# Eight half-tile sums of each group, and the two small operations of a row tile's scale, issued on GpSimd instead of VectorE

## The chip, the cores and the metric

The kernel runs on one core of a Trainium2 chip. The core has TensorE (PE, matrix products into PSUM), VectorE (DVE), ScalarE (ACT), GpSimd (POOL) and SyncE (SP, which issues the DMA transfers here). Each engine runs its own instructions in order, and instructions on different engines are tied together by semaphores. The metric is device microseconds for one execution of the whole kernel. The kernel before took 1449.78 us as the median of 2 runs (1449.72 to 1449.84).

## The reference

```python
# x: (8, 2048, 2048) float32, w: (2048, 2048) float32
def reference(x, w):
    cs = np.cumsum(x, axis=1)
    diff = cs - np.concatenate([zeros, cs[:, :-1, :]], axis=1)
    return np.matmul(diff, w).astype(np.float32)
```

A running sum along the second axis followed by the difference of neighbours gives x back, so what has to be computed is the product of x, seen as a matrix of 16384 rows by 2048 columns, with w.

## The kernel before

**Tiling.** The rows of x are cut into 128 row tiles of 128 rows. The first tiles are multiplied plainly in bf16 (the head), while w is being read. From row tile 4 on, the work is in f16: four row tiles make a group, called g, h, k and l (rows g, g+2, g+1, g+3), and the group's product with w is done with a scheme of Strassen's kind: sums of blocks of x times sums of blocks of w, with fewer products and more additions. The first f16 group (`group_plain`) and the next (`group_half`) are written out by hand. The other 29 groups are made by the class `Group` and form a steady loop.

**One group in the loop.** The half of a row tile that belongs to one half of the inner dimension is a `Part` of 128 x 1024 f16 numbers in the tiles x (`turned_x`). The eight sums that the change concerns combine the parts in place: for the pairs g,k and h,l they are S1 (A21 + A22), S2 (S1 - A11), S4 (A12 - S2) and S3 (A22 - S2, called after S4 in the plan). There are seven large products P1 to P7. P6 and P7 read S2 and S3 directly: each is eight steps (`P6g.0` to `P6g.3`, `P6h.0` to `P6h.3`) of four matmuls, issued from line 609. P1 to P5 go one level deeper: each has four small sums of 128 x 512 (`P1.s1` to `P5.s3`, line 599, 0.42 us each on VectorE) and seven quarter products of four matmuls (line 628), with one or two sums of weights made for them just in time in the tile `flow` (`P2.fp4`, `P5.fp5` and so on, line 955, 128 x 2048). P5 reads S1, P3 reads S4. All of them together are 51 steps of four matmuls in a group. ScalarE (`keep`, line 636) and VectorE (`add`, line 639) gather the products from PSUM into the f32 results c, which SyncE stores (`put`).

**How a row tile comes in.** `load` (SyncE, into one of five f32 buffers F), `weigh` (ScalarE, line 125: the sum of the absolute values of a row), `scale` (lines 142 and 144: a maximum with a tiny number and its reciprocal, 128 x 1), `unit` (GpSimd, line 150, 128 x 2: what the results are multiplied by), `narrow` (ScalarE, line 164: f32 to f16, times the scale, in place), `turn` (SyncE, line 177: two transposing DMAs into the parts). There is one place in x for each of g, h, k and l, so `turn` of the next group waits until TensorE has read the last of this one.

**The order.** Each engine's instructions go in the order in which the kernel asks for them (`after` chains them). In the loop that order is one list written out by hand, `ORDER`, in which every step stands once with the group that it is of (`S1.g+1` is of the group one ahead of `P4.p6+0`). It is one order for all engines, and each engine follows its own part of it. GpSimd's part of the list is, in the kernel before, `unit.h unit.g unit.l unit.k`. VectorE's part around the sums is

```
... P2.s1 P2.s2 P1.m2 P2.s4 S1.g S2.g add.C21h1.q scale.l add.C11g0.v P2.fp4 P2.s3 add.C11g1.q S4.g
add.C11h1.e add.C11h1.q add.C21h0.x S3.g add.C11h0.q P5.fp5 S1.h P5.s1 scale.g P5.s2 P5.s4 S2.h P5.s3
add.C11g1.e P5.fp4 P5.m1 S4.h P3.s1 P3.s2 P5.m2 S3.h P3.s4 P3.s3 add.C22g0.x P3.fp2 add.C12h1.z scale.h ...
```

and TensorE's part in the same stretch is

```
... P1.p3 P1.p4 P2.p2 P6g.0 P2.p6 P6g.1 P2.p5 P6g.3 P2.p7 P6g.2 P5.p1 P2.p4 P2.p3 P7g.0 P7g.1 P5.p2 P5.p5
P5.p6 P6h.2 P6h.1 P6h.3 P6h.0 P5.p7 P7g.2 P7g.3 P5.p4 P5.p3 P7h.0 P3.p2 P3.p1 P7h.2 ...
```

Of the kernel before, what the change touches and what calls it, by code (L numbers as in the profile page):

```python
# [10 lines left out]
def kernel(  # L11
# [6 lines left out]
    nc = tc.nc  # L18
    P = 128
# [10 lines left out]
    f32 = mybir.dt.float32  # L30
    ADD = mybir.AluOpType.add
    SUB = mybir.AluOpType.subtract
    MUL = mybir.AluOpType.mult
    MAX = mybir.AluOpType.max
# [5 lines left out]
    TINY = 1e-34  # L40
# [11 lines left out]
    const = ctx.enter_context(tc.tile_pool(name="const", bufs=1))  # L52
# [19 lines left out]
    uw = const.tile([P, 2], f32, name="uw")  # L72
    uinv = const.tile([P, 2], f32, name="uinv")

    waste = const.tile([P, NH], mybir.dt.uint8, name="waste")
    F = const.tile([P, 5, NH], f32, name="F")
    turned_x = [
# [10 lines left out]
    def after(engine, ask):  # L88
        if engine in last:
            with tc.issue_after(last[engine].ins):  # L90
                said = ask()
        else:
            said = ask()
        last[engine] = said[-1] if isinstance(said, tuple) else said
        return said
# [38 lines left out]
    def scale_of(t):  # L134
        if t < END:
            m2 = sums_of.pop(t)
            m, s = (m2[:, i : i + 1] for i in (2, 3))
            u = m2[:, 4:6]
            scales[t], unit[t] = s, u
            after(  # L140
                "dve",
                lambda: nc.vector.tensor_scalar(m, m2[:, :1], m2[:, 1:2], TINY, ADD, MAX),  # L142
            )
            after("dve", lambda: nc.vector.reciprocal(s, m))  # L144
            sizes[t] = m

    def unit_of(t):
# [38 lines left out]
    with ExitStack() as head:  # L186
# [195 lines left out]
        for ko in range(1, KO - 1):  # L382
# [3 lines left out]
            q = (ko + 1) // KQ  # L386
# [3 lines left out]
            for r in range(PLAIN):  # L390
                if turning and r in (0, PLAIN - 1):
                    a = r // 2
# [23 lines left out]
        def bring(ko):  # L416
            fetch(1, ko)
            cast(1, ko)
            measure(1, ko)
            if ko == AHEAD:  # L420
                scale_of_w(0)
            if ko > AHEAD:
                turn_left(1)
            if ko == 10:
                load(PLAIN, 0)
                load(PLAIN, 1)
                weigh(PLAIN)
                scale_of(PLAIN)
            if ko == 11:
                narrow(PLAIN)  # L430
# [51 lines left out]
        for k in range(KH):  # L482
            block(B12, 0, 1, k, "dve")
            if k == 1:
                scale_of(PLAIN + 2)
            if k % 2:
                if k // 2:
                    finish_row(k // 2)
# [12 lines left out]
        turn(PLAIN + 2)  # L501
        weigh(PLAIN + 1)
        scale_of(PLAIN + 1)
        unit_of(PLAIN + 1)
        narrow(PLAIN + 1)
# [32 lines left out]
    S1 = [S1_all[:, ds(2 * i, 2), :] for i in range(2)]  # L538
    inner = alone([P, 20, NB], f16, "inner")
    flow = alone([P, 4, NB], f16, "flow")  # L540
    S1 = [Part(t) for t in S1]
# [55 lines left out]

    def total(dst, p, q, op):
        after("dve", lambda: nc.vector.tensor_tensor(dst.all, p.all, q.all, op))  # L599


    def steps(to, a, b, first, pieces):
# [59 lines left out]
    def sums_in(a, b, to):  # L662
        a11, a12, a21, a22 = a.half(0), a.half(1), b.half(0), b.half(1)
        s1, s2, s3, s4 = to

        def one():
            total(s1, a21, a22, ADD)
            total(s2, s1, a11, SUB)

        def two():  # L670
            total(s3, a11, a21, SUB)
            total(s4, a12, s2, SUB)

        return one, two, (a11, a12, a22, s1, s2, s3, s4)
# [300 lines left out]
    class Group:  # L975
# [120 lines left out]
        def plan(self):  # L1096
# [25 lines left out]
            v, q, e = "2v", "2q", "2e"  # L1122
# [18 lines left out]

            for a, b in ("gk", "hl"):
                (A11, A12), (A21, A22) = half[a], half[b]
                self.step(f"S1.{a}", total, A21, A21, A22, ADD)
                self.step(f"S2.{a}", total, A11, A21, A11, SUB)
                self.step(f"S4.{a}", total, A12, A12, A11, SUB)
                self.step(f"S3.{a}", total, A11, A22, A11, SUB)

            self.whole("P6", T2, half["g"][0], half["h"][0], *x)
            for n, c in zip(x, ("C12h0", "C12h1", "C12g0", "C12g1")):  # L1150
# [8 lines left out]
            q, e = "3q", "3e"  # L1159
# [26 lines left out]
            q, e = "4q", "4e"  # L1186
# [149 lines left out]
```

## Time and profile before

| what | value |
|---|---|
| median of the runs | 1449.78 us (1449.72 to 1449.84) |
| span of the profiled execution, first to last instruction | 1447.4 us |
| time around the span (median less span) | 2.4 us |
| TensorE busy | 1437.9 us, 99% |
| VectorE busy | 1319.0 us, 91% |
| ScalarE busy | 970.5 us, 67% |
| GpSimd busy | 43.8 us, 3% |
| mean granted TensorE clock | 1.000 |
| one group in the loop | 44.04 us |

The profiled execution has its span as its own time; the runs' median stands 2.4 us above it. The page of the profile gives busy time by engine, then the costliest groups of instructions by source line, with the mean duration of one and the idle time of the engine just before them. The timeline of an engine lists its instructions in order of time with start and duration, neighbours of one kind merged ("x2"); a tiny overlap of neighbours is the pipeline. Steps are found in it by counting along the lists above, since the loop repeats every 44.04 us.

### The profile page before, as it was taken

Reading aid. Unit: us, or ns where it says so; the run is one execution under the profiler, and the core shown is the slowest. Engines: PE = TensorE matmul, PEld = TensorE weight load, DVE = VectorE, ACT = ScalarE, POOL = GpSimd, SP = SyncE. Lnnn points to the kernel's source line nnn. Section 1 sums busy time; section 2 is a strip of 40 time slices with the busy share of each in tenths; the row PEclk is TensorE's granted clock in tenths of the full one; section 3 lists DMA queues with packets and bytes.
Section 4 is the critical chain, followed back from the end, with each engine's and each line's share of the span. In section 5 each row is a group of like instructions: output and inputs, shape, how many; then the busy total and the mean of one; then the engine's idle time right before and its main releaser. Section 6 shows DMA issues by size and latency. Waiting matters only on the chain.

```text
span 1447.4 us, 20191 instructions
## 1 busy us (share of the span) xinstructions
PE 1437.9 (99%) x6686; PEld 651.6 (45%) x6692; DVE 1319.0 (91%) x2310; ACT 970.5 (67%) x1472; POOL 43.8 (3%) x130
## 2 busy tenths in 40 slices
PE   8999999999999999999999999999999999999998
PEld 4444444444444444444444444444444444444443
DVE  4899899999999999999999999999999999999998
ACT  6987566666666776666666667666667766666662
POOL 0011000000000000000000000000000000000000
PEclk9999999999999999999999999999999999999999
DMA  9999788899888898888899888998878998889973
GB/s 363 368 257 298 200 234 232 239 253 253 226 224 239 238 254 245 231 233 236 248 247 232 234 238 233 262 240 234 228 234 240 252 234 239 226 242 248 255 200 127
DMA packets 378199, 351.58 MB, mean 243 GB/s; under 512 B 274800, under 2 KB 274800, under 8 KB 377968
## 3 DMA queue, kind: packets, MB, share of 16 engines
q1 hardware_dynamic: 378096, 350.31, 86.5%
q8 instruction: 52, 0.85, 0.2%
q14 instruction: 51, 0.42, 0.1%
HBM read 150.99 MB, written 134.22 MB: 197 GB/s over the span
## 4 chain that ended last, share of the span: by engine, by line
PE 97%; DMA 2%; DVE 0%; SPq 0%; issue 0%; DVEq 0%
PE b L628 62%; PE b L609 33%; PE b L304 2%; DMA W<-in_w_dram 2%; DMA W<-in_x_dram 0%; DVE c L639 0%; PE b L464 0%; SPq L225 0%; DVE wb L267 0%; SPq L259 0%; DVEq L267 0%; DVEq L639 0%
## 5 line engine op out<-in xcount | busy, mean ns | idle before, releaser
L639 DVE SCALAR_TENSOR_TENSOR c<-b,of,c 128x512 f32<-128x512 f32 x790 | 573.6, 746 | 71.1 <-PE b L628 61.4
L609 PE MATMUL b<-W,x 128*128 128x512 f16 x2144 | 507.1, 379 | 0.0
L636 ACT ACTIVATE c<-b,of 128x512 f32<-128x512 f32 x492 | 312.7, 680 | 220.2 <-PE b L628 113.8
L628 PE MATMUL b<-W,x 128*128 128x512 f16 x1904 | 454.9, 379 | 0.0
L164 ACT ACTIVATE F<-F,of 128x1024 f16<-128x1024 f32 x246 | 282.3, 1148 | 175.6 <-DVE of L144 173.4
L628 PEld LDWEIGHTS <-x 128*128 128x128 f16 x2500 | 244.6, 98 | 295.4 <-issue 1.0
L609 PEld LDWEIGHTS <-x 128*128 128x128 f16 x2144 | 209.7, 98 | 253.3 <-issue 0.5
L125 ACT ACTIVATE waste<-F 128x1024 uint8<-128x1024 f32 x246 | 259.3, 1054 | 8.3 <-DMA F<-in_x_dram 6.2
L628 PEld LDWEIGHTS <-inner 128*128 128x128 f16 x1644 | 160.8, 98 | 194.0
L628 PE MATMUL b<-W,inner 128*128 128x512 f16 x940 | 241.2, 379 | 0.0
L599 DVE TENSOR_TENSOR x<-x,x 128x1024 f16<-128x1024 f16 (+1 forms) x390 | 227.1, 583 | 3.3
L628 PE MATMUL b<-flow,x 128*128 128x512 f16 x584 | 149.9, 379 | 0.0
L628 PE MATMUL b<-inner 128*128 128x512 f16 x472 | 121.1, 379 | 0.0
L955 DVE TENSOR_TENSOR flow<-W 128x2048 f16<-128x2048 f16 x87 | 105.7, 1215 | 0.0
L1053 DVE TENSOR_TENSOR b<-b,c 128x512 f32<-128x512 f32 x116 | 80.4, 693 | 12.7 <-PE b L628 12.7
L150 POOL TENSOR_SCALAR of<-uw,of 128x2 f32<-128x2 f32 x124 | 42.6, 357 | 1299.6 <-DVE of L142 717.1
L955 DVE TENSOR_TENSOR flow<-W,inner 128x2048 f16<-128x2048 f16 x58 | 70.7, 1220 | 0.0
L1046 ACT COPY c<-b 128x512 f32<-128x512 f32 x58 | 33.4, 576 | 51.2 <-PE b L628 51.2
L304 PE MATMUL b<-wb,xP 128*128 128x512 bf16 x234 | 53.2, 379 | 2.2 <-ACT wb L265 1.1
L599 DVE TENSOR_TENSOR inner<-x 128x512 f16<-128x512 f16 x117 | 49.3, 421 | 3.1 <-DMA x<-F 1.0
L1046 ACT COPY b<-b 128x512 f32<-128x512 f32 x87 | 51.2, 589 | 0.2 <-PE b L628 0.2
L599 DVE TENSOR_TENSOR inner<-x,inner 128x512 f16<-128x512 f16 x117 | 49.2, 421 | 2.0
(68 smaller groups left out, 517.5 us busy)
## 6 DMA issues: line engine op xcount, KB each, us to landing
F<-in_x_dram SPq DMA_DIRECT2D x246, 512.0 KB, 5.2
out_dram<-c SPq DMA_DIRECT2D x492, 256.0 KB, 3.0
W<-in_w_dram SPq DMA_DIRECT2D x32, 512.0 KB, 8.4
W<-in_x_dram SPq DMA_DIRECT2D x16, 256.0 KB, 7.8
x<-F SPq DMA_TRANSPOSE x246, 3.4
out_dram<-o SPq DMA_DIRECT2D x5, 256.0 KB, 7.0
out_dram<-wb SPq DMA_DIRECT2D x5, 256.0 KB, 7.0
xP<-in_x_dram SPq DMA_DIRECT2D x1, 1024.0 KB, 6.4
```

Of the source, the lines that this page charges most:

```text
L125: lambda: nc.scalar.activation(waste, where[t][i], ABS, scale=1.0 / ROW, accum_out=sums_of[t][:, i : i + 1],),
L150: after("pool", lambda: nc.gpsimd.tensor_scalar(u, uw, m, None, MUL))
L164: lambda: nc.scalar.activation(narrowed(t)[:, ds(i * NH, NH)], where[t][i], COPY, scale=s),
L304: lambda: nc.tensor.matmul(ps[r][n], xP[:, r, ko, :], wb[h, ko][:, ds(n * NB, NB)], start=(ko == 0), stop=(ko == KO - 1),),
L599: after("dve", lambda: nc.vector.tensor_tensor(dst.all, p.all, q.all, op))
L609: said = nc.tensor.matmul(to[n], a[k], b[k][:, n, :], start=(first and k == 0), stop=(k == KH - 1), skip_group_check=True,)
L628: said = nc.tensor.matmul(to, a[k], b[k], start=(first and k == 0), stop=(k == 3), skip_group_check=True)
L636: after("act", lambda: nc.scalar.activation(c, p, COPY, scale=u))
L639: after("dve", lambda: nc.vector.scalar_tensor_tensor(c, p, u, c, MUL, ADD))
L955: after("dve", lambda: nc.vector.tensor_tensor(in_twos(to), x, y, op))
L1046: after("act", lambda: nc.scalar.copy(c, p))
L1053: after("dve", lambda: nc.vector.tensor_tensor(t, p, s, ADD))
```

## The change

The eight sums S1 to S4 of the loop are asked of GpSimd by a new helper `total_aside`, at the same places of `ORDER`. The sums of the two groups written out by hand stay on VectorE. The two operations of `scale` go to GpSimd too, for every row tile from the first f16 one on, and the reciprocal is written as the power -1, with a constant column of -1.

```diff
+    minus = const.tile([P, 1], f32, name="minus")
+    nc.vector.memset(minus, -1.0)
...
             after(
-                "dve",
-                lambda: nc.vector.tensor_scalar(m, m2[:, :1], m2[:, 1:2], TINY, ADD, MAX),
+                "pool",
+                lambda: nc.gpsimd.tensor_scalar(m, m2[:, :1], m2[:, 1:2], TINY, ADD, MAX),
             )
-            after("dve", lambda: nc.vector.reciprocal(s, m))
+            after(
+                "pool",
+                lambda: nc.gpsimd.tensor_tensor(s, m, minus, mybir.AluOpType.pow),
+            )
...
+    def total_aside(dst, p, q, op):
+        after("pool", lambda: nc.gpsimd.tensor_tensor(dst.all, p.all, q.all, op))
...
-                self.step(f"S1.{a}", total, A21, A21, A22, ADD)
-                self.step(f"S2.{a}", total, A11, A21, A11, SUB)
-                self.step(f"S4.{a}", total, A12, A12, A11, SUB)
-                self.step(f"S3.{a}", total, A11, A22, A11, SUB)
+                self.step(f"S1.{a}", total_aside, A21, A21, A22, ADD)
+                self.step(f"S2.{a}", total_aside, A11, A21, A11, SUB)
+                self.step(f"S4.{a}", total_aside, A12, A12, A11, SUB)
+                self.step(f"S3.{a}", total_aside, A11, A22, A11, SUB)
```

GpSimd's part of the list becomes `unit.h unit.g S1.g S2.g scale.l unit.l unit.k S4.g S3.g S1.h scale.g S2.h S4.h S3.h scale.h scale.k`, where each `scale` is two instructions.

## The prediction

> **What bounds the kernel now.** I read the page first, then the busy time of each engine over the whole loop and over one group.
>
> ```profile
> span 1447.4 us, 20191 instructions
> PE 1437.9 (99%) x6686; PEld 651.6 (45%) x6692; DVE 1319.0 (91%) x2310; ACT 970.5 (67%) x1472; POOL 43.8 (3%) x130
> ```
>
> ```profile
> 160.00:1400.00 1240.00, 1240.00 (x5746) 562.00 (x5744) 1149.98 (x2030) 832.12 (x1265) 30.24 (x111) 1.00 0.87 238
> 635.84:679.88 44.04, 44.04 (x206) 19.96 (x205) 40.79 (x72) 29.61 (x45) 1.09 (x4) 1.00 0.89 239
> ```
>
> Columns of the second fence: window, length, then busy time of TensorE, its weight loads, VectorE, ScalarE and GpSimd, then granted clock. In 1240 us of the loop TensorE is busy 1240.00 us at clock 1.00, so it never stalls: whatever VectorE saves there saves nothing, and every delay that reaches a matmul is added in full, in each of 29 groups of 44.04 us. All idle time of TensorE in the span is 1447.4 - 1437.9 = 9.5 us, less than the 29 us (2%) that a measurement of this kernel can tell from no change. So the question is only which sum comes too late, and by how much.
>
> **What is moved.** The groups of instructions, shapes kept apart (count, busy time, mean ns of one, idle before):
>
> ```profile
> L164 ACT ACTIVATE F<-F,of 128x1024 f16<-128x1024 f32 x246 | 282.3, 1148 | 175.6 <-DVE of L144 173.4
> L599 DVE TENSOR_TENSOR x<-x,x 128x1024 f16<-128x1024 f16 x240 | 164.1, 684 | 1.1
> L150 POOL TENSOR_SCALAR of<-uw,of 128x2 f32<-128x2 f32 x124 | 42.6, 357 | 1299.6 <-DVE of L142 717.1
> L142 DVE TENSOR_SCALAR of<-of 128x1 f32<-128x1 f32 x124 | 25.4, 205 | 4.4 <-ACT waste L125 4.3
> L144 DVE RECIPROCAL of<-of 128x1 f32<-128x1 f32 x124 | 20.3, 164 | 4.3
> ```
>
> 232 of the 240 sums move (29 groups of 8; the other 8 are in the groups written by hand), and 124 scales. VectorE loses 8 x 0.684 + 4 x (0.205 + 0.164) = 6.9 us of its 40.79 per group. That is worth nothing by itself, since TensorE is full.
>
> **What one sum costs on GpSimd (S).** The trace has none. From below the nearest row is VectorE's own 0.684 us. From above I take four times ScalarE's row of one operand of 1024 numbers, 4 x 1.148 = 4.6 us. I choose S = 2.3 us, twice that row: GpSimd's small operations (0.357 us for 128x2 on the average, 0.28 undisturbed, below) cost more than VectorE's (0.205), so it is nearer to the engine that takes one number at a time, and a sum has two operands where ScalarE's instruction has one. The Trainium skill, "GPSIMD Engine Reference", section 3.1, gives 4497 ns for an f32 sum of 2048; half of it, 2.25 us as an estimate, would make the sum below 4.7 us a group in place of 4.9. The scale's two operations I put at 0.3 us each, the row of 128x2 without its waits; the power is not in the trace, and lies between nothing and 1.15 us (ScalarE's long row), 0.85 us more a scale at worst.
>
> **Do GpSimd and VectorE hinder each other?** GpSimd's timeline beside VectorE's, early and in the loop:
>
> ```profile
> 87.47 1.37 POOL L150 TENSOR_SCALAR of<-uw,of 128x2 f32<-128x2 f32 x1 [8.67 <-DVE of L142]
> ...
> 658.30 0.55 POOL L150 TENSOR_SCALAR of<-uw,of 128x2 f32<-128x2 f32 x2 [21.75 <-DVE of L142]
> ```
>
> ```profile
> 87.49 3.68 DVE L591 TENSOR_TENSOR W<-W 128x1024 f16<-128x1024 f16 x6
> ...
> 658.17 0.16 DVE L144 RECIPROCAL of<-of 128x1 f32<-128x1 f32 x1
> 658.28 0.75 DVE L639 SCALAR_TENSOR_TENSOR c<-b,of,c 128x512 f32<-128x512 f32 x1
> ```
>
> The same GpSimd operation takes 0.28 us (two in 0.55) beside an `add`, whose big operand b is in PSUM, and 1.37 us beside sums of two tiles in SBUF: it got through after the second of six. So GpSimd waits for VectorE's two-tile sums, and not for its adds. Whether VectorE's sums wait for GpSimd in turn, no row shows; I forecast that they do, for the whole of S, and price the other case as a rival. The Trainium skill, "SBUF — State Buffer", section "Who interferes with whom", has it so: the pair of ports is taken by whichever comes first for its whole instruction and the other is blocked. The row above agrees for one direction; by this rule the sum is 4.9 us a group, without it 2.4.
>
> **Where a later sum reaches TensorE.** One group, VectorE:
>
> ```profile
> 653.08 1.22 DVE L955 TENSOR_TENSOR flow<-W,S 128x2048 f16<-128x2048 f16 x1
> 654.21 0.42 DVE L599 TENSOR_TENSOR inner<-x 128x512 f16<-128x512 f16 x1
> 654.67 0.42 DVE L599 TENSOR_TENSOR inner<-inner,x 128x512 f16<-128x512 f16 x1
> ...
> 655.61 0.41 DVE L599 TENSOR_TENSOR inner<-x,inner 128x512 f16<-128x512 f16 x1
> 655.94 1.41 DVE L599 TENSOR_TENSOR x<-x,x 128x1024 f16<-128x1024 f16 x2
> ...
> 666.42 1.22 DVE L955 TENSOR_TENSOR flow<-W 128x2048 f16<-128x2048 f16 x1
> 667.55 0.69 DVE L599 TENSOR_TENSOR x<-x,x 128x1024 f16<-128x1024 f16 x1
> 668.28 0.42 DVE L599 TENSOR_TENSOR inner<-x 128x512 f16<-128x512 f16 x1
> ...
> 669.73 1.14 DVE L599 TENSOR_TENSOR x<-x,x 128x1024 f16<-128x1024 f16 x2
> ```
>
> TensorE (P6g.0, P6g.2, P7g.0, P5.p5, and P6h.2 with the P6h steps behind it; a step of four issues in 0.863 us):
>
> ```profile
> 657.78 1.03 PE L609 MATMUL b<-W,x 128*128 128x512 f16 x4
> ...
> 662.96 1.03 PE L609 MATMUL b<-W,x 128*128 128x512 f16 x4
> ...
> 666.42 1.89 PE L609 MATMUL b<-W,x 128*128 128x512 f16 x8
> ...
> 669.01 1.03 PE L628 MATMUL b<-flow,inner 128*128 128x512 f16 x4
> ...
> 670.73 3.62 PE L609 MATMUL b<-W,x 128*128 128x512 f16 x16
> ```
>
> The transpose that brings k's second half (issue, and time to landing), and ScalarE's narrow after the scale of l:
>
> ```profile
> 649.90 2.31 SPq L177 DMA_TRANSPOSE x<-F  x1
> ```
>
> ```profile
> DMA to landing us min/median/max: 4.3/4.3/4.3
> ```
>
> ```profile
> 658.37 2.33 ACT L164 ACTIVATE F<-F,of 128x1024 f16<-128x1024 f32 x2 [0.80 <-DVE of L144]
> ```
>
> A signal between engines I count as 0.1 us (the narrow starts 0.04 us after the reciprocal's end, 658.33). Three places are tight, and the stalls add up because each moves all of TensorE's later steps.
>
> *A, before P6g.0.* S1.g needs k's transpose, landed at 649.90 + 4.3 = 654.2. Two small sums stand on VectorE then, and GpSimd gets through behind the second, at 655.0. S1.g takes S; the small sum of 655.61 slips in behind it (0.35); S2.g takes S and needs S1.g. P6g.0 is ready at 655.0 + S + 0.45 + S + 0.1 = 655.55 + 2S, due at 657.78: late by 2S - 2.23 = **2.4 us**. Now VectorE does both by 657.35, 0.4 us ahead.
>
> *B, before P5.p5.* S3.g overwrites what P6g.2 reads, and P6g.2 ends at 662.96 + 1.03 = 663.99 (all of it moved by A). S3.g is done at 664.1 + S = 666.4, just in time for P7g.0 (666.42 on this clock). S1.h follows until 664.2 + 2S. The sum of weights for P5.p5 (666.42 on VectorE) meets it and waits, or goes first and delays it, which comes to the same: 1.13 more, 0.35 for P5.s1, a signal: 665.78 + 2S, due at 669.01: late by 2S - 3.23 = **1.4 us**.
>
> *C, before P6h.2.* Behind S1.h on GpSimd stands scale.g, which gets through when VectorE's two sums of B are done, at 665.68 + 2S; 0.6 for it, then S2.h: 666.38 + 3S. P6h.2 is due at 670.73 + (2S - 3.23): late by S - 1.12 = **1.2 us**.
>
> The sum is 5S - 6.58 = 4.9 us a group, and 29 x 4.9 = 143 us.
>
> **What is hidden.** S4.g and S4.h feed P3's small sums, whose first matmul is near 679, 5 us and more behind them. S3.h follows the P6h steps (674.35) and P7h.0 comes at 678.50: 4.15 us for S + 0.2. If S were over 3.9 this cover would go. scale.l stands behind S2.g and moves ScalarE's narrow of l from 658.4 to about 661.8, and the transposes and their landing from 664.5 to 668; S1.h then starts at 664.1 + 2.3 + 2.4 = 668.9, so 0.9 us of cover is left there. scale.h and scale.k stand behind S3.h, when ScalarE has idled before (173.4 us in all for the reciprocal). In the head the first scale lies between GpSimd's two reductions over partitions; that costs between nothing and the 9.5 us of TensorE idle again, and I take nothing. GpSimd's own load, 8 x 2.3 + 12 x 0.3 = 22 us of 44, binds nowhere. VectorE keeps 40.79 - 6.9 = 33.9 us of work a group; if each of GpSimd's sums held it up for its whole length that would be 33.9 + 18.4 = 52.3 us, over the 44.04 + 4.9 = 48.9 that A to C give. Adds run on beside GpSimd, so I count nothing for it, and 3.4 us a group (99 us) at worst; the same delay would reach SyncE, where stores wait in one queue for the adds, with the transposes behind them.
>
> The sum stands on one profiled span of 1447.4 us; the runs' median, 1449.8, is 2.4 us above it and I add to that: 1449.8 + 143 = **1593 us**.
>
> **Rivals.**
> 1. *VectorE doesn't wait for GpSimd.* Then S1.g starts at 654.3 and nothing slips between. A becomes 2S - 3.28 = 1.3, B (no weights' sum in the way) 2S - 4.36 = 0.2, C S - 1.47 = 0.8, together 2.4 us, 69 us in all: 1519 us. For it: VectorE's two operations at 87.41 and 87.49 show no mark of GpSimd's. Against: GpSimd clearly waits, and a shared thing seldom yields one way alone.
> 2. *GpSimd's sum is short.* If S is 1.5 us or less, A is at most 0.8, B nothing and C under 0.2: under 1 us a group, under 29 us in all, and at S = 1.1 or below nothing at all: 1450 us, not slower. The price is VectorE's rate (0.684 for two operands) at best; it decides at S = 1.5. For it: f16 operands are half as wide as the f32 that ScalarE reads. Against: GpSimd's small operations.
> 3. *GpSimd's sum is longer*, 3 us: 5 x 3 - 6.58 = 8.4, and 0.7 at P7g.0, of which B's stall has to be taken off; about 8.4 us, 244 us: 1693 us. At the upper bound of 4.6 it would be 16.4 us a group, 1926 us.
>
> **How the numbers follow.** Forecast 0.5, rival 1 0.2, rival 2 0.09, rival 3 0.2; 0.01 for anything faster, which the 9.5 us leave no room for. The range reaches from just under rival 1 to rival 3: 1510 to 1695 us, leaving out S under 1.5 and S over 3, two in ten. Slower by over 2% holds 0.5 + 0.2 + 0.2 = 0.90, within 2% 0.09.
>
> **What would show it.** The new profile's groups give S on GpSimd in line 604 or near it, by the spacing of its starts. A shows as TensorE idle before the L609 step of P6g.0, released by GpSimd, 2 us in each group; B as idle before a step on inner released by VectorE; C as idle before P6h.2, again by GpSimd. Small sums of 128x512 that last far over 0.42 us, and weights' sums over 1.22, show the lock in both directions; if they keep their durations rival 1 holds. If TensorE stays at 44.04 us a group, rival 2 does. The forecast is wrong most of all if S is.

## The result, and the profile after

The changed kernel takes 1680.68 us (median of 2 runs, 1677.18 to 1684.18) against 1449.78 us: a ratio of 1.159, 95% interval 1.158 to 1.161. It is slower by 231 us; the forecast was 143 us slower, 1593 us, with a range of 1510 to 1695.

The page of the changed kernel, in the lines that answer to those of before (its source lines are shifted: the matmuls of P1 to P5 are on 636 now, the whole steps of P6 and P7 on 617, VectorE's sums on 604, GpSimd's on 607, the weights' sums on 963, the merges on 1061):

```profile
span 1675.3 us, 20494 instructions
PE 1502.6 (90%) x6686; PEld 655.9 (39%) x6692; DVE 1379.5 (82%) x1831; ACT 971.5 (58%) x1472; POOL 739.5 (44%) x610
PEclk9989999999999999999999999999999999999999
...
PE 54%; DVE 21%; POOL 14%; issue 6%; DMA 3%; ACT 1%; SPq 0%; POOLq 0%; DVEq 0%; ACTq 0%
```

The same line of the kernel before, and its rows for three weights' sums a group and for the merges:

```profile
PE 97%; DMA 2%; DVE 0%; SPq 0%; issue 0%; DVEq 0%
...
L955 DVE TENSOR_TENSOR flow<-W 128x2048 f16<-128x2048 f16 x87 | 105.7, 1215 | 0.0
L1053 DVE TENSOR_TENSOR b<-b,c 128x512 f32<-128x512 f32 x116 | 80.4, 693 | 12.7 <-PE b L628 12.7
```

The chain that ended last was 97% TensorE before and is 54% now; VectorE and GpSimd have come into it with 21% and 14%. The groups of instructions of the changed kernel, shapes kept apart:

```profile
L607 POOL TENSOR_TENSOR x<-x,x 128x1024 f16<-128x1024 f16 x232 | 517.4, 2236 | 598.9 <-DMA x<-F 171.1 <-PE b L636 118.1 <-PE b L617 101.1
L144 POOL TENSOR_SCALAR of<-of 128x1 f32<-128x1 f32 x124 | 102.9, 830 | 245.4 <-ACT waste L127 245.4
L963 DVE TENSOR_TENSOR flow<-W 128x2048 f16<-128x2048 f16 x87 | 192.9, 2217 | 0.0
L604 DVE TENSOR_TENSOR inner<-x 128x512 f16<-128x512 f16 x117 | 132.7, 1134 | 2.6 <-DMA x<-F 2.6
L604 DVE TENSOR_TENSOR inner<-inner,x 128x512 f16<-128x512 f16 x117 | 100.1, 855 | 3.0
L1061 DVE TENSOR_TENSOR b<-b,c 128x512 f32<-128x512 f32 x116 | 79.7, 687 | 3.8 <-PE b L636 3.8
L148 POOL TENSOR_TENSOR of<-of,minus 128x1 f32<-128x1 f32 x124 | 77.5, 625 | 10.3
```

A sum of 128x1024 takes 2.24 us on GpSimd (2.3 was chosen). VectorE lost 232 sums and 248 small operations and is busy for longer than before, 1379.5 us against 1319.0: two kinds of its small sums went from 0.42 to 1.13 and 0.86 us (a third to 0.56), three weights' sums a group from 1.22 to 2.22, while the merges, whose big operand is in PSUM, stayed at 0.69.

Where the 228 us between the two spans are, by the windows of the loop (length, TensorE busy, ... , granted clock) and by what TensorE waited for in it:

```profile
178.40:1667.40 1489.00, 1337.79 (x5917) 581.96 (x5916) 1247.80 (x1628) 848.05 (x1289) 712.27 (x571) 0.97 0.73 202
```

```profile
PE b L636 <- DVE b L1061: 95.7, 81, 3.3
PE b L617 <- POOL x L607: 34.7, 30, 2.1
PE b L636 <- DVE inner L604: 20.7, 30, 2.6
```

Twenty-nine groups took 1489 us; before they took 29 x 44.04 = 1277. So the loop lost 212 us, 7.3 a group, and the head the other 16 (the loop starts at 178.4 us, not at 162.1). Of the 212 us, 1489.0 - 1337.8 = 151 are waits of TensorE, and 61 are matmuls that take longer: the granted clock is 0.97. The trace's record of the clock has TensorE at half speed for 85 us of the loop, which costs about 37 us (the spacing of the matmuls' starts in it); the rest of the 61 is the modelled tail of the last matmul ahead of a wait.

By step, from the spacing of the matmuls' starts (a stall counts 0.16 us more there than in the waits), mean of 29 groups:

```
            forecast   changed kernel
P1.p4          0          2.60   waits for the merge P1.m2 (VectorE)
P6g.0   (A)   2.4         0.13   waits for S2.g (GpSimd)
P5.p5   (B)   1.4         0.87   waits for P5.s1 (VectorE)
P6h.2   (C)   1.2         1.23   waits for S2.h (GpSimd)
P5.p7          0          0.62   waits for the merge P5.m1
P5.p4          0          0.54   waits for the merge P5.m2
half clock     0          1.3
sum           4.9         7.3
head           0 us       16 us, once
```

One group of it, VectorE, GpSimd and TensorE in order of time:

```profile
693.86 0.69 DVE L1061 TENSOR_TENSOR b<-b,c 128x512 f32<-128x512 f32 x1
694.46 1.21 DVE L963 TENSOR_TENSOR flow<-W,S 128x2048 f16<-128x2048 f16 x1
695.59 2.35 DVE L604 TENSOR_TENSOR inner<-x 128x512 f16<-128x512 f16 x1
697.97 2.22 DVE L604 TENSOR_TENSOR inner<-inner,x 128x512 f16<-128x512 f16 x1
700.11 0.69 DVE L1061 TENSOR_TENSOR b<-b,c 128x512 f32<-128x512 f32 x1
```

```profile
694.55 5.35 POOL L607 TENSOR_TENSOR x<-x,x 128x1024 f16<-128x1024 f16 x2 [12.67 <-DVE b L1061]
```

```profile
700.85 1.87 PE L636 MATMUL b<-flow,x 128*128 128x512 f16 x4 [3.26 <-DVE b L1061]
```

S1.g and S2.g hold GpSimd from 694.55 to 699.90. The two small sums of VectorE that fall in it, P2.s1 and P2.s2, take 2.35 and 2.22 us in place of 0.42 each. Nothing on TensorE needs them yet. But behind them in VectorE's queue stands the merge P1.m2, which has to read a PSUM bank before P1.p4 may add to it: the merge ends at 700.80, and P1.p4 starts at 700.85 after 3.26 us of idling. Its four matmuls then take 1.87 us in place of 1.03: the clock record has half clock from 699.7 to 706.5 us.

### The profile page after: what moved, and what is told of

It reads as the page before. It is cut to its first block, busy times and chain, and to the rows that moved or that the text cites. A ratio compares the mean times of both kernels' runs of the same rounds, so it can differ in the third digit from the quotient of the medians.

```text
span 1675.3 us, 20494 instructions
## 1 busy us (share of the span) xinstructions
PE 1502.6 (90%) x6686; PEld 655.9 (39%) x6692; DVE 1379.5 (82%) x1831; ACT 971.5 (58%) x1472; POOL 739.5 (44%) x610
## 4 chain that ended last, share of the span: by engine, by line
PE 54%; DVE 21%; POOL 14%; issue 6%; DMA 3%; ACT 1%; SPq 0%; POOLq 0%; DVEq 0%; ACTq 0%
PE b L636 37%; PE b L617 17%; DVE inner L604 11%; POOL x L607 10%; DVE b L1061 4%; DVE c L647 3%; POOL of L144 3%; DVE flow L963 2%; DMA W<-in_w_dram 1%; POOL of L148 1%; DVE x L604 1%; DMA W<-in_x_dram 0%; ACT waste L278 0%; DVE W L347 0%; DMA F<-in_x_dram 0%
## 5 line engine op out<-in xcount | busy, mean ns | idle before, releaser
L607 POOL TENSOR_TENSOR x<-x,x 128x1024 f16<-128x1024 f16 x232 | 517.4, 2236 | 598.9 <-DMA x<-F 171.1
L617 PE MATMUL b<-W,x 128*128 128x512 f16 x2144 | 520.9, 386 | 46.7 <-POOL x L607 34.7
L636 PE MATMUL b<-W,x 128*128 128x512 f16 x1904 | 467.1, 386 | 13.7 <-DVE b L1061 13.6
L636 PE MATMUL b<-flow,x 128*128 128x512 f16 x584 | 161.0, 401 | 82.1 <-DVE b L1061 82.1
L144 POOL TENSOR_SCALAR of<-of 128x1 f32<-128x1 f32 x124 | 102.9, 830 | 245.4 <-ACT waste L127 245.4
L963 DVE TENSOR_TENSOR flow<-W 128x2048 f16<-128x2048 f16 x87 | 192.9, 2217 | 0.0
L604 DVE TENSOR_TENSOR inner<-x 128x512 f16<-128x512 f16 x117 | 132.7, 1134 | 2.6 <-DMA x<-F 2.6
L604 DVE TENSOR_TENSOR x<-x,x 128x512 f16<-128x512 f16 (+1 forms) x158 | 68.2, 433 | 62.1 <-POOL x L607 58.5
L604 DVE TENSOR_TENSOR inner<-inner,x 128x512 f16<-128x512 f16 x117 | 100.1, 855 | 3.0
L148 POOL TENSOR_TENSOR of<-of,minus 128x1 f32<-128x1 f32 x124 | 77.5, 625 | 10.3
L604 DVE TENSOR_TENSOR inner<-x,inner 128x512 f16<-128x512 f16 x117 | 65.4, 559 | 2.0
```

The costliest lines, as they stand in the source:

```text
L144: lambda: nc.gpsimd.tensor_scalar(m, m2[:, :1], m2[:, 1:2], TINY, ADD, MAX),
L148: lambda: nc.gpsimd.tensor_tensor(s, m, minus, mybir.AluOpType.pow),
L607: after("pool", lambda: nc.gpsimd.tensor_tensor(dst.all, p.all, q.all, op))
L617: said = nc.tensor.matmul(to[n], a[k], b[k][:, n, :], start=(first and k == 0), stop=(k == KH - 1), skip_group_check=True,)
L636: said = nc.tensor.matmul(to, a[k], b[k], start=(first and k == 0), stop=(k == 3), skip_group_check=True)
L963: after("dve", lambda: nc.vector.tensor_tensor(in_twos(to), x, y, op))
```

## The experiments

Each was run once, beside the kernel before on the same chip (1449.6 us, 1450.3 for the last two).

**The two halves of the change.** First the sums alone on GpSimd, then the scale alone.

```diff
 # sums only: scale_of as before, on VectorE
-                lambda: nc.gpsimd.tensor_scalar(m, m2[:, :1], m2[:, 1:2], TINY, ADD, MAX),
+                lambda: nc.vector.tensor_scalar(m, m2[:, :1], m2[:, 1:2], TINY, ADD, MAX),
...
 # scale only: the sums as before
-                self.step(f"S1.{a}", total_aside, A21, A21, A22, ADD)
+                self.step(f"S1.{a}", total, A21, A21, A22, ADD)
```

> The changed kernel with the scale's two operations back on VectorE; the eight sums stay on GpSimd. Theory (a chain of late sums plus VectorE held up by GpSimd's reads): the stalls before P1.p4 and P5.p5 stay (2.6 and 0.9 us a group), the one before P6h.2 (1.2 us) goes, since in the changed kernel S2.h starts 2.3 us after S1.h ends with the scale between; about 1635 us (1610 to 1660). Rival (the scale is harmless where it is): 1675 us or more, P6h.2 still late.

> The changed kernel with the eight sums back on VectorE; the scale's two operations stay on GpSimd. Theory: the scale costs about 1.0 us there in place of 0.37, and ScalarE, idle before its narrow, covers it; TensorE stays full, 1450 us (1447 to 1456). Rival (the scale's wait for VectorE's sums, up to 1.5 us, moves the transposes and with them S1): 1465 to 1490 us with stalls before P6g.0 or P5.p1.

Sums only: 1700.0 us, more than the whole change. The head is back (the loop starts at 161.9 us), but a group takes 52.7 us. The stall before P6h.2 went, as expected, and the one before P1.p4 shrank from 2.6 to 1.9 us; those before P5.p5 and P5.p6 grew from 0.9 to 2.7 + 1.2 us, which was not expected. GpSimd, then VectorE in the sums-only run:

```profile
709.16 9.53 POOL L604 TENSOR_TENSOR x<-x,x 128x1024 f16<-128x1024 f16 x4 [0.97 <-PE b L614]
```

```profile
714.37 2.33 DVE L601 TENSOR_TENSOR inner<-x 128x512 f16<-128x512 f16 x1
...
716.95 2.02 DVE L601 TENSOR_TENSOR inner<-inner,x 128x512 f16<-128x512 f16 x1
719.00 0.42 DVE L601 TENSOR_TENSOR inner<-x,inner 128x512 f16<-128x512 f16 x1
```

The loop of the sums-only run, columns as above:

```profile
161.90:1690.40 1528.50, 1366.70 (x5918) 590.92 (x5917) 1300.21 (x1854) 850.84 (x1289) 571.68 (x345) 0.94 0.72 196
```

Without the scale between them, S3.g, S1.h, S2.h and S4.h follow one another on GpSimd for 9.5 us, and P5.s1 and P5.s2, which P5.p5 and P5.p6 need at once, get in only one at a time: 2.33 and 2.02 us. The stalls before P5.p7 and P5.p4 went in exchange. All in all the waits are about the same as in the changed kernel (1528.5 - 1366.7 = 162 us against 151), but the clock is 0.94 against 0.97: half speed for 174 us of the loop against 85. So the scale on GpSimd costs the head and gives something back in the loop.

Scale only: 1465.0 us. That is the rival's time, but without the stalls that either theory speaks of: the loop keeps 44.04 us a group without a stall, and all 16 us are lost in the head, since the loop starts at 178.2 us. TensorE in the head of the scale-only run:

```profile
68.88 3.61 PE L469 MATMUL b<-W,xP 128*128 128x512 f16 x16 [0.94 <-ACT wb L337]
...
88.14 1.46 PE L617 MATMUL b<-W,x 128*128 128x512 f16 x3 [8.59 <-DMA x<-F]
...
92.32 8.43 PE L617 MATMUL b<-W,x 128*128 128x512 f16 x29 [2.71 <-ACT x L478]
```

and GpSimd there:

```profile
66.33 0.38 POOL L294 PARTITION_ALL_REDUCE uw<-wtop  x1 [7.29 <-DVE wtop L293]
77.35 4.93 POOL L155 TENSOR_SCALAR of<-uw,of 128x2 f32<-128x2 f32 x1 [10.64 <-DVE W L518]
81.66 1.35 POOL L144 TENSOR_SCALAR of<-of 128x1 f32<-128x1 f32 x1
```

Behind the second reduction over partitions GpSimd does nothing for 10.6 us. The view names a sum of VectorE as what ended this, but the unit reads nothing of that sum, and the last VectorE result that it does read was there at 66.9 us. The trace has two reconfigurations of the engine right behind the reduction; whether they cause the idle stretch was not tested. Its next instruction, a unit, then meets VectorE's run of two-operand sums and takes 4.93 us. Only then comes the scale of row tile 6, at 81.7 us in place of 68.1, and narrow, transposes and the matmuls behind them are as late. The kernel before has the same idle stretch (10.09 us from the reduction to the unit), but there nothing that TensorE needs soon was queued behind it. A half-clock stretch of 13.7 us (82.8 to 96.4 us) goes with it.

**The scale in the loop alone.**

```diff
+            engine, where_to = ("dve", nc.vector) if t < PLAIN + 4 else ("pool", nc.gpsimd)
             after(
-                "pool",
-                lambda: nc.gpsimd.tensor_scalar(m, m2[:, :1], m2[:, 1:2], TINY, ADD, MAX),
+                engine,
+                lambda: where_to.tensor_scalar(m, m2[:, :1], m2[:, 1:2], TINY, ADD, MAX),
             )
 # the reciprocal, or the power, likewise
```

> The kernel before with the scale's two operations on GpSimd for the row tiles of the loop alone; those of the first eight row tiles stay on VectorE, and all sums too. Theory (the 15 us that the scale costs all arise in the head, where it stands on GpSimd behind the reduction over partitions and a unit that starts 10 us later): 1450 us (1447 to 1453), the loop starts at 162 us as before. Rival (the scale costs in the loop too, hidden by the way the group's time is counted): 1460 us or more.

1454.7 us, above the expected range: 44.04 us a group, so in the loop the scale costs nothing by itself; 10 of the head's 16 us are gone. The loop starts at 168.0 us and not at 162: one stall of 3.67 us at 123.6 us and half-clock time are left. The edit does not cover the whole head, since row tiles 8 to 11 belong to the second group written by hand and their scales still stand on GpSimd. In the trace one of these starts at 106.02 us beside VectorE's two-operand sums and takes 3.40 us, ScalarE's narrow behind it starts at 110.97 us in place of 107.09, and the stall waits for ScalarE. That they cause it is therefore likely, but no run tests it.

**Does VectorE wait for GpSimd's reads?** All sums and scales are on VectorE here, and GpSimd is given work that only takes its time.

```diff
+    def total_and_read(dst, p, q, op):
+        total(dst, p, q, op)
+        for i in range(8):
+            some = dst.all[:, i // 4, ds(i % 4 * 128, 120)]
+            after("pool", lambda: nc.gpsimd.tensor_tensor(aside, some, some, ADD))
...
 # with fills, instead:
+        after("pool", lambda: nc.gpsimd.tensor_copy(aside[:, :2], dst.all[:, 0, :2]))
+        for _ in range(10):
+            after("pool", lambda: nc.gpsimd.memset(aside, 0.0))
...
 # reading a weights' block (the copy of two numbers kept, and 8 sums, or 4):
+            some = T2[0][:, i // 4, ds(i % 4 * 128, 120)]
+            after("pool", lambda: nc.gpsimd.tensor_tensor(aside, some, some, ADD))
```

> The kernel before (all sums and scales on VectorE), with eight added GpSimd sums of 128x120 behind each S sum, which read its result and write to a tile that nobody reads: GpSimd reads SBUF for some 2 to 3 us where the changed kernel does, and nothing waits for it. Theory (VectorE's two-operand sums wait while GpSimd reads): small sums and weights' sums on VectorE stretch by 0.3 us and more on the average, VectorE passes its 44 us a group, 1520 to 1720 us. Rival (only GpSimd waits, VectorE never does): VectorE's sums keep 0.42, 0.68 and 1.22 us, 1450 us.

> As the one with added reads, but behind each S sum GpSimd copies two numbers a partition of its result and then fills the spare tile (128x120) ten times with zero: GpSimd works as long, and writes SBUF but hardly reads it. Theory (it is GpSimd's reading that holds VectorE's two-operand sums): VectorE's sums keep their times, 1450 us (1447 to 1465). Rival (any GpSimd work, or issuing it, holds VectorE): as long as with the added reads.

> As the run with added fills, but in place of the fills GpSimd makes eight sums of 128x120 that read a block of weights which nothing writes in the loop: GpSimd reads, and VectorE has no result of it to wait for. Theory (VectorE's two-operand sums wait while GpSimd reads, for one instruction at a time): VectorE's sums that meet them stretch by up to 0.3 to 0.5 us, its adds and merges do not; 1450 to 1500 us. Rival (VectorE never waits; what the run with added reads lost came from VectorE waiting by semaphore to overwrite what was being read): VectorE's sums keep 0.42, 0.68 and 1.22 us, 1450 us.

> The run with reads of a weights' block, with four in place of eight, so that GpSimd is busy behind each S sum as long as in the run with fills (about 2.4 us) and its queue doesn't fall behind. Theory (VectorE's two-operand sums wait for GpSimd's reads, one instruction of 0.4 us at a time, and the 310 us of the two earlier runs with reads came from VectorE waiting by semaphore on a queue that had fallen behind): small sums 0.43 to 0.5 us on the average against 0.42 with the fills, most of the loss gone, 1450 to 1490 us. Rival (reading alone, by its share of the time, costs TensorE): about half the loss of eight, 1600 us.

The fills took 1449.1 us, the kernel before's own time, with GpSimd busy over 560 us. The reads took 1757.8 us and the reads of the weights 1760.9, both longer than expected, and four of them in place of eight 1467.5.

The two long runs say nothing clean. GpSimd's extra sums came out at 0.5 us each, eight of them behind every S sum make 34 us of a group with the copy, its queue fell behind, and VectorE waited by semaphore to overwrite what GpSimd had yet to read; the expectation of the first was wrong in that nothing waited for them. The longest waits of the run that reads the weights show it (the copy of two numbers is on line 607):

```profile
DVE x L601 <- POOL aside L607: 293.3, 58, 7.3
```

With four sums that wait is gone, and what is left is in the length of VectorE's own sums. VectorE's groups with four reads, and with the fills:

```profile
L653 DVE SCALAR_TENSOR_TENSOR c<-b,of,c 128x512 f32<-128x512 f32 x790 | 572.9, 745 | 55.9 <-PE b L642 43.7 <-PE b L623 0.8 <-POOL aside L610 0.3
L601 DVE TENSOR_TENSOR x<-x,x 128x1024 f16<-128x1024 f16 x240 | 178.5, 744 | 1.1
L601 DVE TENSOR_TENSOR inner<-x,inner 128x512 f16<-128x512 f16 x117 | 56.5, 483 | 2.0
```

```profile
L652 DVE SCALAR_TENSOR_TENSOR c<-b,of,c 128x512 f32<-128x512 f32 x790 | 573.6, 746 | 70.9 <-PE b L641 61.3 <-PE b L622 0.8 <-POOL aside L609 0.3
L601 DVE TENSOR_TENSOR x<-x,x 128x1024 f16<-128x1024 f16 x240 | 164.2, 684 | 1.1
L601 DVE TENSOR_TENSOR inner<-x,inner 128x512 f16<-128x512 f16 x117 | 49.2, 421 | 2.0
```

The run came out in the expected range (its groups are 0.63 us longer than before). Reads stretch VectorE's two-operand sums (0.684 to 0.744, 0.421 to 0.483 us on the average) and leave its adds as they are; fills stretch nothing. So VectorE waits for GpSimd, and it is GpSimd's reading that it waits for. The Trainium skill, "SBUF — State Buffer", section "Who interferes with whom", says both; these runs agree.

**Is P1.p4 late through the queue on VectorE, and does the clock hang on it?** The merge is put ahead of the two small sums.

```diff
-    P1.m1+1 P4.p7+0 P1.fp4+1 put.C21g0+0 load.g+2 P2.s1+1 P2.s2+1 P1.p7+1
-    P1.m2+1 P2.s4+1 P2.p1+1 ...
+    P1.m1+1 P4.p7+0 P1.fp4+1 put.C21g0+0 load.g+2 P1.p7+1
+    P1.m2+1 P2.s1+1 P2.s2+1 P2.s4+1 P2.p1+1 ...
```

> The changed kernel with one change of order: VectorE's merge P1.m2, for which P1.p4 waits, stands ahead of the small sums P2.s1 and P2.s2 instead of behind them. Theory 1 (P1.p4 is late because the merge queues behind small sums that GpSimd's S1.g and S2.g hold up): the stall of 2.6 us a group before P1.p4 goes, about 0.8 us comes before P6g.0; and, as no stall then fills most of one 3.41 us window, TensorE keeps its full clock, which gives back another 1.5 us a group: about 1590 us (1570 to 1615). Theory 2 (the forecast's: S2.g itself is late for P6g.0): the stall only moves to P6g.0, 2.4 us, 1660 us or more. If the loss of clock doesn't hang on the long stalls: about 1630 us at the same clock of 0.97.

1594.6 us, as the first theory expected and 86 less than the changed kernel, with nothing else touched. The stall before P1.p4 is gone; 0.98 us stands before P6g.0; the other four are the same to 0.03 us. The loop and its clock in this run:

```profile
178.40:1585.00 1406.60, 1304.06 (x5918) 571.92 (x5917) 1235.09 (x1628) 848.00 (x1289) 711.37 (x571) 1.00 0.78 214
```

The waits fell by 151 - 103 = 49 us, the matmuls' busy time by 34 us. A part of the loss therefore was clock, and it went with the long stall (half clock for 7 us of the loop in place of 85). The windows of 3.41 us in which the clock record changes agree: over the loops of the changed kernel and the sums-only run, a window at full clock in which TensorE idled for 2.14 us or less (by the modelled starts of its matmuls) never had a half-clock window behind it, save one at 2.05; from 2.20 us on it always did.

**Are some of the sums free?**

```diff
-                self.step(f"S1.{a}", total_aside, A21, A21, A22, ADD)
+                self.step(f"S1.{a}", total, A21, A21, A22, ADD)
 # S2 and S3 likewise, and the scale; S4 stays on GpSimd
```

> The kernel before with S4.g and S4.h alone on GpSimd (two of the eight sums; scale on VectorE). Both have over 5 us before a matmul needs them. Theory (what counts is whether a sum, or a VectorE sum behind it, is due soon): TensorE stays full, 1450 us (1447 to 1456), although VectorE's sums that meet S4 stretch by up to 2.2 us. Rival (each sum on GpSimd costs its share, 231 / 8 = 29 us): 1505 us.

1462.8 us: the two S4 cost 13 us, not nothing and not 58. A group takes 44.5 us, and all of the increase is one stall of 0.46 us before P5.p7. In the S4-only run:

```profile
677.77 2.49 DVE L960 TENSOR_TENSOR flow<-W 128x2048 f16<-128x2048 f16 x1
680.19 0.69 DVE L1058 TENSOR_TENSOR b<-b,c 128x512 f32<-128x512 f32 x1
```

```profile
PE b L633 <- DVE b L1058: 8.6, 28, 1.9
```

S4.h itself has time, but the weights' sum P5.fp4 meets it, takes 2.49 us in place of 1.22, and the merge P5.m1 behind it is what P5.p7 waits for. It is the case of P1.m2 once more.

**Half of each sum.**

```diff
     def total_aside(dst, p, q, op):
-        after("pool", lambda: nc.gpsimd.tensor_tensor(dst.all, p.all, q.all, op))
+        d, p, q = dst.all, p.all, q.all
+        after("pool", lambda: nc.gpsimd.tensor_tensor(d[:, 0], p[:, 0], q[:, 0], op))
+        after("dve", lambda: nc.vector.tensor_tensor(d[:, 1], p[:, 1], q[:, 1], op))
 # scale on VectorE
```

> The run with the sums alone on GpSimd, but GpSimd makes only the first 512 columns of each of the eight sums and VectorE the other 512; scale on VectorE. A sum on GpSimd should take 1.15 to 1.2 us. By the forecast's terms (5S - 6.58, none below zero) A is 0.1 to 0.2 us, B nothing, C 0.1: about 0.2 us a group, 1455 us. If instead what counts is how long VectorE's queue stands behind a sum that GpSimd holds up, the stalls of the sums-only run shrink by one or two times 1.1 us each: P1.p4 1.9 to about 0.6, P5.p5 2.7 to about 0.5, P5.p6 to 0.1: 1.2 us a group, full clock, 1485 us. If the loss were by the number of moved instructions and not by their length: 1690 us.

1503.1 us. The row of GpSimd's halves, and TensorE's longest waits:

```profile
L605 POOL TENSOR_TENSOR x<-x,x 128x512 f16<-128x512 f16 x232 | 316.0, 1362 | 790.1 <-DMA x<-F 298.6 <-PE b L616 207.6 <-DVE b L1060 100.3
```

```profile
PE b L635 <- DVE b L1060: 21.8, 25, 1.3
PE b L635 <- DVE inner L601: 21.4, 29, 1.9
```

GpSimd's half takes 1.36 us with its waits; 0.9 us stands before P1.p4 and 0.9 before P5.p5, the clock is full, a group takes 45.9 us. The forecast's terms miss it (1455), the queue on VectorE has the places right and the size too small (1485). The loss does go with the length of a sum: 250 us at 2.31 us a sum (sums only), 53 at 1.36.

## Why the prediction was right, and where it was not

The direction was right, and so was its ground: sums that come late on GpSimd, or that hold VectorE up, stop TensorE in every group. That 1681 us lies in the range is in part luck. The range reaches up to 1695 for a sum longer than 2.3 us, and the sum was not longer; the time beyond 1593 us came from terms that the forecast put at nothing.

*TensorE is full, and each delay counts in every group.* Right: the loop lost 212 of the 228 us, in the same five places of nearly every group, and 6.9 us a group less work on VectorE bought nothing.

*S = 2.3 us.* Right: 2.24 us, or 2.1 where two follow one another undisturbed. The Trainium skill's figure ("GPSIMD Engine Reference", section 3.1), halved, was 2.25. The scale's two operations were put at 0.3 us each and took 0.83 and 0.63, waits included. Only scale.g counts for a matmul in the loop, in C: in the group shown 2.3 us pass between the end of S1.h and the start of S2.h, where the forecast had 2.1.

*VectorE waits for GpSimd for the whole of S.* Right, and rival 1 falls: small sums of 2.35 us in the changed kernel, and the runs with four reads and with fills.

*A, P6g.0 waits 2.4 us for S2.g.* The size was nearly right (2.6 + 0.1 us), but by luck, since the step was wrong. The forecast had the two small sums P2.s1 and P2.s2 go first and hold GpSimd up. In the trace S1.g comes at or ahead of them, they are the ones that wait, and the merge behind them makes P1.p4 late, two steps ahead of P6g.0. The changed kernel with the merge first shows the true A: 0.98 us. There S1.g starts when the transpose has landed, as in rival 1, whose 2S - 3.28 gives 1.2 us at S = 2.24. What the forecast left out is VectorE's queue behind a blocked sum; it looked only at the consumers of the sums that moved and of the blocked ones, not at the instruction behind.

*B 1.4 and C 1.2 us.* Measured 0.87 and 1.23. B's mechanism is in the trace: in the group shown P5.fp5 meets S1.h and takes 3.00 us in place of 1.22; S was 2.13 us there, with which B's own term gives 1.0. C's mechanism (S2.h behind the scale) is borne out by the sums-only run, in which it goes.

*Not in the sum.* P5.p7 and P5.p4, 0.62 and 0.54 us: merges behind blocked sums, as at P1.p4. The clock, 1.3 us a group. And the head: "I take nothing", with 9.5 us as the bound, where it cost 16 us; the bound fell too, because it counted idle time of TensorE that was there, and not what could be added. That is 34, 38 and 16 us, less 5 by A and B together, about the 85 between 143 and 228.

*What was hidden.* S4 and S3.h were called hidden. Their own consumers do come late enough. But S4.h blocks the weights' sum P5.fp4, ahead of the merge for P5.p7 (0.46 us a group with the two S4 alone), and S3.h, at 724.16 in the group shown, runs with P3.s1, which takes 2.18 us and stands ahead of the merge for P5.p4. Only S4.g left no stall that was seen.

## What to carry to other kernels

Where two engines hold each other up, the instruction that comes too late need not be the one that was blocked (here P1.p4, P5.p7 and P5.p4 each waited for a merge that stood behind it): read the blocked engine's queue past it, and look for the first instruction that the full engine needs soon. On a loop in which TensorE never idles, work taken off VectorE is worth nothing, so an operation may move to GpSimd only if neither it nor anything behind the VectorE sums that it blocks is due within its length; and stalls should be kept apart and short, since long ones cost clock as well. A small operation that is moved takes its place in another queue everywhere it is issued, in the head too: price it there by what stands ahead of it.

## What the runs showed of the hardware that was not expected

TensorE fell to half clock for whole windows of 3.41 us after windows in which it idled for 2.2 us or more (with 2.14 us or less it did so once), well under a full window; 85 us of the changed kernel's loop and 174 us of the sums-only loop passed so. The Trainium skill, "TensorE: Matmul & The Clock Gate", Part 1, gives the window's length, and a whole idle window as what it takes to fall; the length agrees, the rest is less here.

After the second reduction over partitions GpSimd did nothing for 7.05 to 10.64 us before its next ordinary instruction in the twelve traces: 10.09 us in the kernel before, 10.53 in the changed one, 7.05 in the run with fills. What it does in that time, and why the time varies, no run shows.

GpSimd filling a tile (ten fills of 128x120 behind each of 232 sums, 459 us in all) disturbed neither VectorE nor the time. Four small sums in their place, which read, made VectorE's two-operand sums longer and cost 17 us.
